# The second norm of two feed-forward blocks, rearranged to one tile per unit of the output projection

## The chip, the cores and the metric

The kernel runs on one core of a Trainium2 chip. The metric is the device time of one execution in microseconds (us), the median of several. A core has five engines with a queue each, worked off in order: TensorE (PE, matrix products; its weight loads are shown apart as PEld), VectorE (DVE), ScalarE (ACT), GpSimd (POOL) and SyncE (SP, which here issues most of the DMA transfers). Engines wait for each other through semaphores. Matrix products are written to PSUM, in eight banks of 128 x 512 fp32 values; all other operands lie in SBUF.

## The reference, cut to what matters

One decoder layer over 2048 prompt positions and 32 sample positions (8 sequences of 4), model width 1024. What concerns the change is the end of the layer:

```python
x = x + jnp.concatenate([att, u * gate], axis=-1) @ w_out          # output projection, residual
h = x * rsqrt(mean(x * x, -1) + EPS) * norm2_g                     # second norm
x = x + (silu(h @ w_gate) * (h @ w_up)) @ w_down                   # feed-forward, width 2816
y = rmsnorm(x, final_g)
```

All of it is fp32. The kernel keeps fp32 accuracy with products of a reduced type: each operand is split into a high half (a rounded copy) and a low half (the operand less its high half), and each product is made of three matmuls, high by high, high by low and low by high.

## The kernel before

The first part (projections, attention, gating) isn't touched. After it the 16 prompt tiles of 128 positions go through in three blocks: tiles 0 to 5, 6 to 11, and 12 to 15 with the sample rows as a fifth, small tile. `next_block` (L1856) runs blocks two and three. Within it a block goes through these steps on TensorE:

1. the last down products of the block before (`downs`);
2. `open_unit` (L1789) for each tile: the first 512 columns of the output projection, 8 steps of 3 matmuls, into one bank per tile (`B.banks`);
3. `second_unit` (L1794) for each tile: the other 512 columns, 24 matmuls (16 for the sample tile) into two alternating banks (`ps_o`);
4. the transposes of the second norm, woven between the units of step 3;
5. the feed-forward over 22 chunks of 128 hidden columns. Its products come as seven products a chunk (`product`, L1564) of sums of quarters of the tiles (a scheme of Strassen's kind: quarters b11, b12, b21, b22 and the sums t1 to t4), so the transposed and scaled tile isn't enough: the norm must also make the four sums and split all seven terms into halves. Block two does its first chunk in two parts, tiles 0 to 3 and tiles 4 and 5.

Every engine works in the order in which the program issues to it. The order around step 3 comes from a small planner: `tick()` (L1267) advances a counter, and `later(n, fn, ...)` (L1263) puts a function off by n ticks. A unit has two ticks, one ahead of each half. At the ticks of step 3 the splits of the first chunk's weights also fall due (`prepare`, L1538: high half on ScalarE at L1513, low half at L1517 on VectorE or GpSimd), and, in block two's second unit and ahead of it, the ends of the last open units (`first_end`, L1851).

The second norm of one tile, as it stands, is four functions:

- `norm2_a` (L1401), issued right after the unit's residual add (`out_end`, L1375): the square of the second half of the row with its sum, on ScalarE (L1405). The first half's sum was made at `first_end`. The scratch output of the square goes where the tile's projection input lay.
- `rms_b` (L1385), one tick later: two small VectorE instructions and the root (Sqrt) on ScalarE (L1389).
- `norm2_b` (L1416), two ticks later: the reciprocal and its refinement on VectorE (`newton`, L142 to L146), then the scaled tile on ScalarE (L1420), into `pair`, which has two buffers.
- `norm2_c` (L1425), `put_off` ticks after that (2, or 1 for a block's last three tiles): eight transposes on TensorE into the two banks of `ps_t` (L1434), three copies out of PSUM on ScalarE (L1449, L1450, L1452), low halves and four sums on VectorE (L1451, L1442 to L1445, L1454), and the high halves of the sums on ScalarE with their low halves on GpSimd (`split_sb`, L135 and L138). The sums lie in `zn` buffers, of which there are three; a tile takes two.

The tick puts `norm2_c` of a tile into the queues two units behind its own, ahead of the root or the scaling of later tiles. In block three the sample tile is the first in the order, but its `norm2_c` stands behind all units (L1896), for its operands take columns 64 to 67 of every quarter of every tile, and the projection inputs of tiles that have not been multiplied lie across these columns (`place_of`, L1323).

Of the kernel before, what the change touches and what calls it, by code (L numbers as in the profile page):

```python
# [64 lines left out]
def hymba_step(ctx: ExitStack, tc: tile.TileContext, A: dict, O: dict):  # L65
# [100 lines left out]
    def zn_tile():  # L166
        return rp.tile([P, 512], F32, name="zn", tag="zn", bufs=3)
# [1105 lines left out]
    class Block:  # L1273
# [6 lines left out]
            self.acc, self.wo, self.cat, self.late, self.h, self.open, self.s1 = {}, {}, {}, {}, {}, {}, {}  # L1280

        def place(self):
            self.X = []
            for nm in ("xh2", "xl2"):
                t_ = fc.tile([P, 6 * 28 * 64], F32R, name=nm, tag=nm)
                self.X.append(t_[:, 0:self.nt * 28 * self.w].rearrange("p (i n) -> p i n", i=self.nt))
            self.ops = [x.rearrange("p i (j k w) -> p i j k w", j=7, k=4) for x in self.X]

    def acc_tile(B, i):
# [32 lines left out]

    def place_of(B, i):  # L1323

        return tuple(x[:, i, 0:KD * P].rearrange("p (s t) -> p s t", t=P) for x in B.X)


# [94 lines left out]

            later(put_off, norm2_c, B, i, xn)

    def norm2_c(B, i, xn):  # L1425

        n = B.rows[i]
        hi, lo_ = B.ops
        pts = []
        for kk in range(2):  # L1430
            pt = ps_t()
            for k in range(4):
                c0 = (kk * 4 + k) * P
                pe.transpose(pt[:, k * P:k * P + n], xn[:n, c0:c0 + P], ident[:n, :n])  # L1434
            pts.append(pt.rearrange("p (k t) -> p k t", k=4)[:, :, 0:n].rearrange("p k (z t) -> p z k t", z=2))
        (b11, b12), (b21, b22) = ((p_[:, 0], p_[:, 1]) for p_ in pts)
        sums = [zn_tile()[:, 0:2 * 4 * (n // 2)].rearrange("p (j k t) -> p j k t", j=2, k=4) for _ in range(2)]
        (t1, t2), (t3, t4) = ((s_[:, 0], s_[:, 1]) for s_ in sums)

        def sums_of():  # L1440

            dve.tensor_sub(t1, t4, b11)  # L1442
            dve.tensor_sub(t3, b22, t4)
            dve.tensor_sub(t2, b22, t1)
            dve.tensor_sub(t4, b21, t2)  # L1445

        if n == P:
            at_ = lambda x, j0, j1: x[:, i, j0:j1, :, 0:64]
            act.activation(at_(hi, 0, 1)[:, 0], b11, AF.Copy)  # L1449
            act.activation(t4, b12, AF.Copy)  # L1450
            dve.tensor_sub(at_(lo_, 0, 1)[:, 0], b11, at_(hi, 0, 1)[:, 0].bitcast(F32))  # L1451
            act.activation(at_(hi, 1, 3), pts[1], AF.Copy)  # L1452
            sums_of()
            dve.tensor_sub(at_(lo_, 1, 3), pts[1], at_(hi, 1, 3).bitcast(F32))  # L1454
            for s_, j in zip(sums, (3, 5)):
                split_sb(at_(hi, j, j + 2), at_(lo_, j, j + 2), s_)
        else:
            act.activation(t4, b12, AF.Copy)
            sums_of()
            for j, x in enumerate((b11, b21, b22, t1, t2, t3, t4)):  # L1460
                at_ = lambda y: y[:, :, j, :, 64:].rearrange("p i k c -> p k i c")
                x = x.rearrange("p k (i c) -> p k i c", i=B.nt)
                split_sb(at_(hi), at_(lo_), x, eng_lo=dve)

# [389 lines left out]
    def next_block(B, downs, finals):  # L1856
# [26 lines left out]
        for i in order:  # L1883
            open_unit(B, i)
        first_operands(B)
        for i in order[:-1] if B.last else order:
            second_end(B, i, second_unit(B, i), 1 if i in tiles[-3:] else 2)
        if B.last:
            i = order[-1]
            out_end(B, i, 1, second_unit(B, i))  # L1890
            s1 = B.s1.pop(i)
            act.activation(B.X[0][:, i, 512:1024], B.acc[i][:, 512:1024], AF.Square, accum_out=s1[:, 3:4])
            rms_b(s1, P, s1[:, 3:4])
            norm2_b(B, i, s1, 2)
            tick()
            norm2_c(B, n - 1, B.xns)  # L1896
            tick()

    for bi, B in enumerate(blocks):
        if bi == 0:  # L1900
# [180 lines left out]
```

## Time and profile before

| what | value |
|---|---|
| median of 3 runs | 2550.32 us (2549.67 to 2557.51) |
| profiled execution, its own time | 2553.33 us |
| span of its profile, first to last instruction | 2551.4 us |
| TensorE busy | 2447.2 us, 96% of the span |
| VectorE, ScalarE, GpSimd busy | 1275.1, 1129.6, 1292.2 us |
| mean granted clock of TensorE | 0.984 |
| block two, first second unit to the first chunk's second part | 1533.0 to 1589.7 us |
| block three, first second unit to the end of the first chunk's second product | 2113.3 to 2161.2 us |

In the profile a row of a timeline has the start in us from the span's start, the duration in us, the engine, the line, the operation, the output and inputs by name, the shapes, a count of merged instructions, and in brackets the idle time ahead of it with the instruction that ended it. A row of a table of stretches has the stretch and its length, then busy time and number of instructions of PE, PEld, DVE, ACT and POOL, the granted clock of TensorE, the share of the DMA engines that was busy and the GB/s that they moved. Matmuls are pipelined, so the duration of one is longer than the distance between two.

### The profile page before, as it was taken

The page shows a single profiled execution, that of the slowest core. Times are in us where ns is not written, and L with a number is a line of the kernel's source. Part 1 is how long each engine was busy: PE and PEld are TensorE (multiplying, and loading weights), DVE is VectorE, ACT ScalarE, POOL GpSimd, SP SyncE. Part 2 cuts the span into 40 slices and gives each one's busy share as a digit, 9 for nine tenths or more (in the row PEclk, how much of TensorE's full clock was granted, in tenths as well). Part 3 has the DMA queues.
Part 4 walks back from the last instruction along what each step waited for, and adds up shares of the span by engine and source line. Part 5 has one row for each costly group of instructions (what it writes and reads, how often), then busy time and mean ns, then how long its engine had stood idle before and what let it go on. Part 6 is the DMA issues. An engine that isn't in the chain of part 4 may idle for free.

```text
span 2551.4 us, 39141 instructions
## 1 busy us (share of the span) xinstructions
PE 2447.2 (96%) x14022; PEld 2120.1 (83%) x14022; DVE 1275.1 (50%) x2598; ACT 1129.6 (44%) x2438; POOL 1292.2 (51%) x1012
## 2 busy tenths in 40 slices
PE   8999999999999898999999999999999998999997
PEld 6777786667888678899899988999999986999996
DVE  4448674216777644443444465444444465444445
ACT  6414333226666556545445355332323345444432
POOL 2116442004777636667677543553645534666662
PEclk9999999999999899999999999999999998999998
DMA  8964735675554463536546471563544543665552
GB/s 260 281 220 150 255 115 164 200 252 197 174 178 151 116 205 112 182 128 198 169 143 201 139 220 62 203 214 128 204 163 160 203 152 122 224 206 192 197 193 106
DMA packets 292149, 455.37 MB, mean 178 GB/s; under 512 B 28695, under 2 KB 160968, under 8 KB 286836
## 3 DMA queue, kind: packets, MB, share of 16 engines
q1 hardware_dynamic: 285108, 440.82, 52.7%
q10 hardware_dynamic: 6848, 12.06, 1.6%
q8 instruction: 111, 1.82, 0.3%
q14 instruction: 82, 0.67, 0.1%
HBM read 365.07 MB, written 157.84 MB: 205 GB/s over the span
## 4 chain that ended last, share of the span: by engine, by line
PE 55%; POOL 9%; issue 7%; ACT 4%; DVE 4%; DMA 2%; SPq 0%; POOLq 0%; ACTq 0%; DVEq 0%
PE ps_o L1647 13%; PE ps_m L1576 8%; PE ps_m L1575 8%; PE ps_m L1574 8%; POOL op L1517 3%; PE ps_s L853 2%; PE ps_o L908 2%; DMA ab_d<-pair 2%; ACT fr L1485 1%; PE ps_t L880 1%; PE ps_s L932 1%; POOL pair L1497 1%; POOL pair L1506 1%; POOL fr L1500 1%; POOL dw L138 1%
## 5 line engine op out<-in xcount | busy, mean ns | idle before, releaser
L1517 POOL TENSOR_TENSOR op<-fr,op 128x512 fp32r<-128x512 f32 x385 | 488.3, 1297 | 313.2 <-ACT op L1513 291.6
L1574 PE MATMUL ps_m<-xh,op 128*128 128x384 f32 (+3 forms) x1904 | 605.2, 318 | 0.0
L1575 PE MATMUL ps_m<-xl,op 128*128 128x384 f32 (+3 forms) x1904 | 604.2, 317 | 0.9 <-POOL xl L138 0.9
L1576 PE MATMUL ps_m<-xh,op 128*128 128x384 f32 (+3 forms) x1904 | 604.6, 318 | 0.0
L1647 PE MATMUL ps_o<-dw,hw 128*128 128x512 f32 x2040 | 484.0, 392 | 15.7 <-DVE acc L1649 14.4
L1647 PEld LDWEIGHTS ps_o<-dw,hw 128*128 128x128 f32 x2040 | 379.5, 188 | 98.6 <-DVE acc L1649 20.7
L1575 PEld LDWEIGHTS ps_m<-xl,op 128*128 128x128 f32 x1904 | 360.3, 189 | 4.8 <-POOL xl L138 1.1
L1574 PEld LDWEIGHTS ps_m<-xh,op 128*128 128x128 f32 x1904 | 360.7, 189 | 4.0
L1576 PEld LDWEIGHTS ps_m<-xh,op 128*128 128x128 f32 x1904 | 360.1, 189 | 0.1
L1649 DVE TENSOR_TENSOR acc<-acc,ps_o 128x512 f32<-128x512 f32 (+1 forms) x362 | 247.1, 686 | 214.8 <-PE ps_o L1647 214.8
L1614 ACT ACTIVATE ps_t<-zn 128x384 f32<-128x384 f32 (+1 forms) x126 | 58.3, 463 | 462.1 <-DVE zn L1597 361.9
L1513 ACT ACTIVATE op<-fr 128x512 fp32r<-128x512 f32 x396 | 235.7, 623 | 24.4 <-DMA fr<-ab_d 19.7
L138 POOL TENSOR_TENSOR dw<-fd,dw 128x1024 fp32r<-128x1024 f32 x66 | 158.5, 2402 | 121.7 <-ACT dw L135 121.7
L318 PE MATMUL ps_s<-wh,xh 128*128 128x512 f32 x480 | 199.7, 416 | 10.6 <-ACT xh L135 6.0
L319 PE MATMUL ps_s<-wl,xh 128*128 128x512 f32 x480 | 191.7, 399 | 1.8 <-DVE wl L226 1.8
L320 PE MATMUL ps_s<-wh,xl 128*128 128x512 f32 x480 | 191.3, 399 | 0.0
L1517 POOL TENSOR_TENSOR op<-pair,op 128x512 fp32r<-128x512 f32 x63 | 81.4, 1301 | 116.4 <-ACT op L1513 116.4
L318 PEld LDWEIGHTS ps_s<-wh,xh 128*128 128x128 f32 x480 | 92.5, 193 | 54.2 <-issue 23.7
L536 POOL TENSOR_TENSOR pr<-kv,qb 96x512 f32<-96x512 f32 x32 | 47.2, 1479 | 178.1 <-DMA qb<-zs_d 61.6
L1624 ACT ACTIVATE hw<-ps_t 128x384 fp32r<-128x384 f32 (+1 forms) x126 | 56.1, 453 | 175.1 <-DVE ps_t L1620 174.1
L924 POOL CAST sq<-k 128x512 fp32r<-128x512 f32 x32 | 34.0, 1062 | 164.3 <-PE ps_s L319 164.3
L320 PEld LDWEIGHTS ps_s<-wh,xl 128*128 128x128 f32 x480 | 92.3, 192 | 20.6 <-DVE xl L138 0.3
(456 smaller groups left out, 4296.6 us busy)
## 6 DMA issues: line engine op xcount, KB each, us to landing
fr<-ab_d SPq DMA_DIRECT2D x308, 256.0 KB
fd<-in_w_down_dram SPq DMA_DIRECT2D x66, 512.0 KB
out_ks_dram<-in_cache_k_dram SPq DMA_DIRECT2D x56, 512.0 KB
out_vs_dram<-in_cache_v_dram SPq DMA_DIRECT2D x56, 512.0 KB
ab_d<-fr SPq DMA_DIRECT2D x88, 256.0 KB
raw<-in_w_in_dram SPq DMA_DIRECT2D x72, 256.0 KB
qk_d<-pair SPq DMA_DIRECT2D x64, 256.0 KB
ab_d<-pair SPq DMA_DIRECT2D x63, 256.0 KB
```

The lines of the kernel that those rows point to most:

```text
L138: (eng_lo or pool).tensor_sub(lo, src, hi.bitcast(F32))
L318: pe.matmul(o[j], xh[:, k, :], wh, start=(k == 0), stop=False)
L319: pe.matmul(o[j], xh[:, k, :], wl, start=False, stop=False)
L320: pe.matmul(o[j], xl[:, k, :], wh, start=False, stop=(k == KD - 1))
L1513: act.activation(ops[f, j][0], ab[f][j], AF.Copy)
L1517: (pool if f or j in POOL_LOW else dve).tensor_sub(lo_, ab[f][j], hi.bitcast(F32))
L1574: pe.matmul(out, wh[:, ks], xh[:, :, k], start=(k == 0), stop=False)
L1575: pe.matmul(out, wh[:, ks], xl[:, :, k], start=False, stop=False)
L1576: pe.matmul(out, wl[:, ks], xh[:, :, k], start=False, stop=(k == 3))
L1614: act.activation(g, c, AF.Silu)
L1647: pe.matmul(ps[0:nr], l_, r_[:, cs], start=(z == 0 and y == 0), stop=(z == FC - 1 and y == len(pairs) - 1))
L1649: dve.tensor_add(B.acc[i][0:nr, cs], B.acc[i][0:nr, cs], ps[0:nr])
```

## The change

`norm2_c` is cut into three parts: `norm2_t`, the transposes, which can now be given their banks; `norm2_v`, the copies out of PSUM; and `norm2_s`, the low halves, sums and splits. A new function `chain` issues, for tile i whose unit has just been issued: the residual add, the square, `rms_b`, the copies of the tile in front, the refinement of the root, the scaling of tile i, and then the sums and splits of the tile in front. Nothing of that is put off by ticks.

In `next_block` the loop over the units issues a unit, then the transposes of the tile in front, then `chain`. Every other tile's transposes go into the banks `ps_m` 0 and 1, which the open units have left, and the rest into `ps_t` as before. The last tile of block two is finished four ticks later, behind three products of the first chunk, with the banks of `ps_o`; the last tile of block three at once, with its low halves on VectorE and not on GpSimd, and the ring of product banks is set so that the first product takes `ps_m` 2. In block three the sample tile's `second_end` comes first, as before, but its `norm2_c` stands behind the first prompt tile's unit and chain. So that it can, the projection inputs of block three's tiles 1 to 3 move to the end of the operand buffers, which that block leaves free (`B.rest`).

```diff
         def place(self):
-            self.X = []
+            self.X, self.rest = [], []
             for nm in ("xh2", "xl2"):
                 t_ = fc.tile([P, 6 * 28 * 64], F32R, name=nm, tag=nm)
                 self.X.append(t_[:, 0:self.nt * 28 * self.w].rearrange("p (i n) -> p i n", i=self.nt))
+                self.rest.append(t_[:, self.nt * 28 * self.w:])
...
     def place_of(B, i):
 
+        if B.last and i:
+            return tuple(x[:, (i - 1) * D:i * D].rearrange("p (s t) -> p s t", t=P) for x in B.rest)
         return tuple(x[:, i, 0:KD * P].rearrange("p (s t) -> p s t", t=P) for x in B.X)
...
-    def norm2_c(B, i, xn):
+    def norm2_t(B, i, xn, banks=None):
 
         n = B.rows[i]
-        hi, lo_ = B.ops
         pts = []
         for kk in range(2):
-            pt = ps_t()
+            pt = banks[kk]() if banks else ps_t()
...
+        return pts
+
+    def norm2_v(B, i, pts):
+
+        n = B.rows[i]
+        (b11, b12), _ = ((p_[:, 0], p_[:, 1]) for p_ in pts)
+        sums = [zn_tile()[:, 0:2 * 4 * (n // 2)].rearrange("p (j k t) -> p j k t", j=2, k=4) for _ in range(2)]
+        if n == P:
+            hi = B.ops[0][:, i, :, :, 0:64]
+            act.activation(hi[:, 0], b11, AF.Copy)
+        act.activation(sums[1][:, 1], b12, AF.Copy)
+        if n == P:
+            act.activation(hi[:, 1:3], pts[1], AF.Copy)
+        return sums
+
+    def norm2_s(B, i, pts, sums, eng_lo=None):
+
         (b11, b12), (b21, b22) = ((p_[:, 0], p_[:, 1]) for p_ in pts)
...
+        if B.rows[i] == P:
+            hi, lo_ = (x[:, i, :, :, 0:64] for x in B.ops)
+            dve.tensor_sub(lo_[:, 0], b11, hi[:, 0].bitcast(F32))
+        dve.tensor_sub(t1, t4, b11)
+        dve.tensor_sub(t3, b22, t4)
+        dve.tensor_sub(t2, b22, t1)
+        dve.tensor_sub(t4, b21, t2)
+        if B.rows[i] == P:
+            dve.tensor_sub(lo_[:, 1:3], pts[1], hi[:, 1:3].bitcast(F32))
             for s_, j in zip(sums, (3, 5)):
-                split_sb(at_(hi, j, j + 2), at_(lo_, j, j + 2), s_)
...
+                split_sb(hi[:, j:j + 2], lo_[:, j:j + 2], s_, eng_lo=eng_lo)
+            return
...
+    def norm2_c(B, i, xn, banks=None, eng_lo=None):
+        pts = norm2_t(B, i, xn, banks)
+        norm2_s(B, i, pts, norm2_v(B, i, pts), eng_lo)
+
+    def chain(B, i, ps, ahead):
+
+        out_end(B, i, 1, ps)
+        s1 = B.s1.pop(i)
+        act.activation(place_of(B, i)[0][:, 4:8], B.acc[i][:, 512:1024].rearrange("p (s t) -> p s t", t=P), AF.Square,
+                       accum_out=s1[:, 3:4])
+        rms_b(s1, P, s1[:, 3:4])
+        if ahead:
+            sums = norm2_v(B, *ahead)
+        r = rms_c(s1, P)
+        xn = square_tile()
+        act.activation(xn, B.acc[i], AF.Copy, scale=r)
+        if ahead:
+            norm2_s(B, *ahead, sums)
+        return xn
...
         first_operands(B)
-        for i in order[:-1] if B.last else order:
-            second_end(B, i, second_unit(B, i), 1 if i in tiles[-3:] else 2)
         if B.last:
-            i = order[-1]
-            out_end(B, i, 1, second_unit(B, i))
...
-            norm2_c(B, n - 1, B.xns)
-            tick()
+            second_end(B, n - 1, second_unit(B, n - 1))
+        two = lambda fn, *a: [lambda: fn(*a[0:1]), lambda: fn(*a[1:2])]
+        front = None
+        for i in tiles:
+            ps = second_unit(B, i)
+            ahead = None
+            if front:
+                ahead = (front[0], norm2_t(B, *front, two(ps_m, 0, 1) if (front[0] + B.last) % 2 else None))
+            front = i, chain(B, i, ps, ahead)
+            if B.last and i == tiles[0]:
+                norm2_c(B, n - 1, B.xns)
+        if B.last:
+            norm2_c(B, *front, eng_lo=dve)
+            turn[3] = 1
+        else:
+            later(4, norm2_c, B, *front, two(ps_o))
```

30 lines of the change are left out of this document (4 added, 26 removed).

## The prediction

> **What bounds the kernel now.** I read the page first, then a table of stretches around the two stages that the change touches, then TensorE's timeline in them, then the rows of the engines that TensorE waits for.
>
> ```profile
> PE 2447.2 (96%) x14022; PEld 2120.1 (83%) x14022; DVE 1275.1 (50%) x2598; ACT 1129.6 (44%) x2438; POOL 1292.2 (51%) x1012
> ```
>
> TensorE is the bound over the span. The stretches, by TensorE busy time, the other engines, granted clock and DMA share:
>
> ```profile
> 1572.00:1589.70 17.70, 14.48 (x100) 14.28 (x101) 9.30 (x26) 9.05 (x18) 5.02 (x4) 0.81 0.00 1
> 2113.30:2145.50 32.20, 30.11 (x137) 23.72 (x135) 15.47 (x45) 16.73 (x34) 9.30 (x8) 0.95 0.38 132
> 2145.50:2161.20 15.70, 7.60 (x42) 6.37 (x40) 8.10 (x30) 10.12 (x26) 5.14 (x5) 0.67 0.00 1
> ```
> ```profile
> 1590.00:1650.00 60.00, 60.00 (x354) 57.07 (x354) 26.36 (x50) 22.53 (x44) 31.75 (x23) 1.00 0.54 184
> 2161.20:2220.00 58.80, 58.80 (x422) 56.07 (x421) 27.95 (x65) 28.54 (x64) 43.70 (x32) 1.00 0.63 215
> ```
>
> Right behind each stage TensorE is full at clock 1.00. In the second norms it is not, and the clock falls to 0.81 and 0.67. So time won there should reach the end. TensorE in block two (a unit is the 24 matmuls of one tile's second half of the output projection; T(i) the eight transposes of tile i; q0 to q6 the seven products of the first feed-forward chunk):
>
> ```profile
> 1532.99 0.39 PE L1367 MATMUL ps_o<-woh,xh 128*128 128x512 f32 x1
> ...
> 1546.59 1.03 PE L1434 MATMUL ps_t<-ident,pair 128*128 128x128 f32 x8
> ...
> 1565.26 1.09 PE L1434 MATMUL ps_t<-ident,pair 128*128 128x128 f32 x8 [2.23 <-ACT pair L1420]
> ...
> 1571.91 1.09 PE L1434 MATMUL ps_t<-ident,pair 128*128 128x128 f32 x8
> 1572.76 0.36 PE L1574 MATMUL ps_m<-xh,op 128*128 128x256 f32 x1
> ...
> 1579.09 1.97 PE L1434 MATMUL ps_t<-ident,pair 128*128 128x128 f32 x8 [3.22 <-ACT pair L1420]
> 1580.71 0.56 PE L1574 MATMUL ps_m<-xh,op 128*128 128x256 f32 x1
> ...
> 1589.81 0.28 PE L1575 MATMUL ps_m<-xl,op 128*128 128x128 f32 x1
> ```
>
> T(3) waits 2.23 us and T(5) 3.22 us for the scaled tile (pair); after the second wait everything runs at about half speed. Prices: two and a half units from 1532.99 to 1546.59, so 5.44 us a unit; T 0.85 us (1571.91 to 1572.76), or 1.62 us at the low clock (1579.09 to 1580.71); q0 and q1 end at 1579.09 - 3.22 = 1575.87 with 0.16 us of drain, so 1.45 us a product. The same in block three, where tile 4 is the sample tile S:
>
> ```profile
> 2113.32 0.39 PE L1372 MATMUL ps_o<-woh,cats 128*64 128x512 f32 x1
> ...
> 2116.95 0.39 PE L1367 MATMUL ps_o<-woh,xh 128*128 128x512 f32 x1
> ...
> 2136.61 1.09 PE L1434 MATMUL ps_t<-ident,pair 128*128 128x128 f32 x8 [2.08 <-ACT pair L1420]
> ...
> 2144.69 1.03 PE L1434 MATMUL ps_t<-ident,pair 128*128 128x128 f32 x8
> ...
> 2150.67 0.60 PE L1434 MATMUL ps_t<-ident,xns 32*128 32x32 f32 x4 [4.94 <-DVE zn L1442]
> 2154.16 2.16 PE L1434 MATMUL ps_t<-ident,pair 128*128 128x128 f32 x8 [1.16 <-DVE xl L138]
> 2155.96 0.57 PE L1574 MATMUL ps_m<-xh,op 128*128 128x272 f32 x1
> ...
> 2159.88 0.39 PE L1575 MATMUL ps_m<-xl,op 128*128 128x272 f32 x1 [0.88 <-POOL xl L138]
> ```
>
> T(1) waits for its tile; T(S) and then T(3) wait for readers of the two transpose banks; q1 waits for GpSimd's low halves.
>
> **Why the scaled tile is late.** VectorE in block two, around tile 3, and ScalarE's scaling of it:
>
> ```profile
> 1557.60 0.68 DVE L1378 TENSOR_TENSOR acc<-acc,ps_o 128x512 f32<-128x512 f32 x1
> ...
> 1563.12 0.15 DVE L142 RECIPROCAL s<-s 128x1 f32<-128x1 f32 x1
> ```
> ```profile
> 1564.06 1.15 ACT L1420 ACTIVATE pair<-acc,s 128x1024 f32<-128x1024 f32 x1 [0.72 <-DVE s L146]
> ```
>
> From the residual add to the scaled tile it takes 1565.21 - 1557.60 = 7.6 us, because the root's four small instructions stand behind the sums of an earlier tile. Block three's last tile has that chain free of sums:
>
> ```profile
> 2144.89 0.69 DVE L1378 TENSOR_TENSOR acc<-acc,ps_o 128x512 f32<-128x512 f32 x1 [2.87 <-PE ps_o L1369]
> ...
> 2147.04 0.16 DVE L142 RECIPROCAL s<-s 128x1 f32<-128x1 f32 x1 [0.27 <-ACT s L1389]
> ...
> 2147.74 0.21 DVE L146 TENSOR_SCALAR s<-s 128x1 f32<-128x1 f32 x1
> ```
> ```profile
> 2146.80 0.20 ACT L1389 ACTIVATE s<-s 128x1 f32<-128x1 f32 x1 [0.47 <-DVE s L1388]
> 2148.05 1.15 ACT L1420 ACTIVATE pair<-acc,s 128x1024 f32<-128x1024 f32 x1 [1.04 <-DVE s L146]
> ```
>
> Counted from the transposes that follow the unit (2144.69), the add starts at 0.2, the root (Sqrt) ends at 2.3, its refinement at 3.3, the scaling at 4.5 us.
>
> **The change, part by part.** (1) Order within a unit. Each unit's chain now comes whole, with T of the tile in front ahead of it on TensorE. Put into the chain are that tile's three copies out of PSUM (after the root, before the scaling); its sums follow on VectorE. Their cost, from tile 3 before:
>
> ```profile
> 1566.01 0.38 ACT L1449 ACTIVATE xh<-ps_t 128x256 fp32r<-128x256 f32 x1 [0.19 <-PE ps_t L1434]
> ...
> 1566.56 0.61 ACT L1452 ACTIVATE xh<-ps_t 128x512 fp32r<-128x512 f32 x1
> 1568.16 1.15 ACT L135 ACTIVATE xh<-zn 128x512 fp32r<-128x512 f32 x2 [0.99 <-DVE zn L1444]
> ```
> ```profile
> 1566.70 0.42 DVE L1451 TENSOR_TENSOR xl<-ps_t,xh 128x256 fp32r<-128x256 f32 x1 [2.09 <-ACT zn L1450]
> ...
> 1568.50 0.68 DVE L1454 TENSOR_TENSOR xl<-ps_t,xh 128x512 fp32r<-128x512 f32 x1
> ```
> ```profile
> 1568.87 2.54 POOL L138 TENSOR_TENSOR xl<-zn,xh 128x512 fp32r<-128x512 f32 x2 [3.48 <-ACT xh L135]
> ```
>
> Copies 1.16 us, sums 2.48 us, two high halves 1.15 us starting 1.46 us after the sums, two low halves on GpSimd 0.7 us later, 2.54 us. In the new order the copies run from 2.3 to 3.5, the scaling to 4.65; TensorE asks for that tile after T and the next unit, at 0.85 + 5.44 = 6.3. Slack 1.6 us, so no wait. VectorE starts the sums at 3.3 and ends at 5.8; one weight low half of 128x512, priced like L1454 at 0.68, makes it 6.5, when the next add is due (6.3 + 0.2). ScalarE: high halves to about 5.9, two weight high halves, priced like the pair of L135 at 1.15, to 7.1, next square at 7.2. Both engines just fit; a few tenths over eat slack and are not seen by TensorE. No instruction is added, no DMA is moved.
>
> (2) Block two ends with T(4), q0, q1, q2, then T(5): TensorE asks for T(5) at 0.85 + 4.35 = 5.2 against 4.65. No wait. VectorE then works off tile 5's sums behind q1 and q2, and q4's second add, which frees q3's bank, comes about 12 us after T(4) began, when TensorE wants that bank: 0.3 us. New time of the first 128-wide product: 1532.99 + 6 x 5.44 + 6 x 0.85 + 7 x 1.45 + 0.3 = 1581.2, against 1589.7 before. **Gain 8.5 us.**
>
> (3) Block three, sample tile moved ahead of unit 1. TensorE wants T(S) at 2116.95 + 5.44 = 2122.4, but
>
> ```profile
> 2122.45 1.14 ACT L1420 ACTIVATE xns<-acc,s 32x1024 f32<-32x1024 f32 x1
> ```
>
> ends at 2123.6, and nothing ahead of it moves: a new wait of 1.2 us. T(S) costs at most the 0.85 us of a whole tile. Its small splits, 2.4 us alternating between ScalarE and VectorE at the end of the stage before, now lie under unit 1. For this the layout puts the projection inputs of tiles 1 to 3 elsewhere; same transfers, other addresses, no cost. Unit 3 then ends at 2123.65 + 0.85 + 3 x 5.44 + 2 x 0.85 = 2142.5.
>
> (4) Block three's tail. Nothing is left to put ahead of T(3). From T(2) at 0: T(3) at 4.7 (an idle of 3.7 us, longer than block two's 3.22, so I take the low clock), ending at 6.3. Tile 2's first low half on GpSimd ends at 6.7, and tile 3's second copy needs that zn buffer (three buffers, two a tile), so its first low product operand is there at 7.5; q0, at the low clock before (from 2155.96 to 2159.88 - 0.88 less the drain, 2.8 us), ends at 10.3; tile 3's low halves are on VectorE now, the one that q1 wants at 10.2; q1 (1.45 x 272/256 = 1.54 us) ends at 11.9, at 2154.4. Before, it ended at 2159.88 + 11/12 x 1.54 = 2161.3. **Gain 6.9 us.**
>
> (5) Other banks. In block two TensorE's waits name only the scaled tile: worth nothing there. In block three the banks and the move of S remove the waits of 4.94 and 1.16 us, counted in (4). The product banks 0 and 1 that T(1) and T(3), or T(0) and T(2), use are read out 0.7 us or more before q0 writes, and after T(2) the ring is set so that q0 takes banks 2 and 3 first: no wait.
>
> Sum 15.4 us. The profiled execution took 2553.33 us around its span of 2551.4, 3.0 us over the median; the median 2550.3 less 15.4 is **2534.9 us**.
>
> **The clock.** Two stretches of 3.41 us ahead of the first drops, and one where there was none:
>
> ```profile
> 1574.48:1577.89 3.41, 1.39 (x12) 1.18 (x10) 2.97 (x12) 1.63 (x5) 1.84 (x2) 1.00 0.00 0
> ```
> ```profile
> 2134.26:2137.67 3.41, 1.32 (x11) 1.06 (x10) 1.60 (x6) 2.50 (x6) 2.49 (x2) 1.00 0.00 0
> ```
> ```profile
> 1560.82:1564.23 3.41, 2.21 (x10) 1.50 (x8) 3.27 (x11) 1.69 (x4) 1.33 (x2) 1.00 0.00 0
> ```
>
> TensorE busy 1.3 to 1.4 us of such a stretch brought the low clock, 2.2 us did not; a gap of 1.2 us (part 3) should not. The Trainium skill, "TensorE: Matmul & The Clock Gate" ("Part 1: The HAM clock gate"), has the clock halve after an idle window of 3.4 us; by it the gap of 2.08 us would have been free, which this trace denies. The Trainium skill, same page ("Part 4: PE-mode transpose"), also says that transposes do not count as busy for the gate, which no stretch here separates; by that sentence the low clock of the tail would last into q1 and q2, and the time would be some 2 us later, an estimate from that page, at 2537, inside the forecast's own range.
>
> **Rivals.** *ScalarE or VectorE paces the units* (0.2). For: part 1 leaves them tenths. Against: 1.6 us of slack per unit. If hops and the weight halves stretch a unit by 2.5 us, four units of block two and two of block three lose 0.9 us each, 5.4 us: 2540. *The gain doesn't reach the end* (0.1, half of it for block three alone). If GpSimd, 43.70 of 58.80 us busy behind block three, sets the next chunks, block three's 6.9 us are given back: 2541.8; were both stages, no change. Against: TensorE is full in both stretches after. *The order on the engines stays as crowded as it is* (0.05): the change then doesn't do what it says, and T(3) and T(5) go on waiting as the 7.6 us chain has them wait, 2550. Against: the emission order is written out, and the root stands ahead of the sums in it. *Slower* (0.04): the chain stays at tile 3's 7.6 us or longer behind copies that wait for a zn buffer, and each wait over 2 us brings the low clock. Block three's wait of 2.08 us cost 1.6 us more at the low clock (0.05 of 32.20 us), 3.7 a unit; eight units lose 30 us against 15 won: 2565. It decides once a chain ends 8.3 us after T instead of 4.65. Against: only tile 3's second copy meets a buffer still in use by the working of part 4.
>
> **How the numbers follow.** As worked out 0.61, within 2531 to 2538.5: a gain up to 4 us larger if the tail keeps its clock (1.5 us) and GpSimd's buffer and the S wait cost nothing (2 us), up to 3.6 us smaller if half clock lasts to q2 and T(5) waits 1 us. With the first two rivals the range is **2531 to 2543**. What a measurement can tell from no change is 0.3%, 7.7 us: faster 0.61 + 0.2 + 0.05 = 0.86, same 0.05 + 0.05 = 0.1, slower 0.04.
>
> **What would show it.** Between the units of block two no idle of TensorE and clock 1.00 up to the 128-wide products; the root's RECIPROCAL ahead of the sums on VectorE in each unit; T(S) behind unit 0 with a wait of about 1.2 us; one idle of 3 to 4 us ahead of T(3) and one low-clock stretch. Wrong would be a wait for pair ahead of T(0) to T(2), a low clock in block two, or TensorE under 97% busy in the 60 us behind a stage.

## The result, and the profile after

The changed kernel takes 2536.91 us (median of 4 executions, 2534.39 to 2537.98) where the kernel before took 2549.99 (4 executions beside it): a ratio of 0.9943, 95% interval 0.9924 to 0.9961 (the comparison's own estimate; the quotient of the two medians is 0.9949). Two more comparisons of the same kernel, with more executions, gave 0.9938 (0.9921 to 0.9956) and 0.9946 (0.9924 to 0.9967). The forecast was 2534.9 us in a range of 2531 to 2543. One execution of a later experiment ran at a mean granted clock of 0.61 and is left out of its comparison.

By stages the profiled execution (2534.39 us, span 2532.2) says more than the total. A stage starts at its first matmul of a second unit; block two's ends at the first 128-wide product, block three's at VectorE's add behind q1. The kernel before ended them here:

```profile
1589.75 0.22 PE L1574 MATMUL ps_m<-xh,op 128*128 128x128 f32 x1
```
```profile
2161.63 0.44 DVE L1586 TENSOR_TENSOR raw<-raw,ps_m 128x272 f32<-128x272 f32 x1 [2.77 <-PE ps_m L1576]
```

The same marks in the timelines of TensorE and VectorE after, with the transposes T(1), T(4) and T(5) of block two, and T(S), T(2) and T(3) of block three:

```profile
1530.17 0.39 PE L1370 MATMUL ps_o<-woh,xh 128*128 128x512 f32 x1
...
1547.39 1.03 PE L1436 MATMUL ps_m<-ident,pair 128*128 128x128 f32 x8
...
1566.39 1.03 PE L1436 MATMUL ps_t<-ident,pair 128*128 128x128 f32 x8
...
1571.58 1.03 PE L1436 MATMUL ps_o<-ident,pair 128*128 128x128 f32 x8
...
1578.74 0.30 PE L1603 MATMUL ps_m<-xh,op 128*128 128x128 f32 x1 [0.38 <-DVE zn L1624]
...
2102.00 0.39 PE L1375 MATMUL ps_o<-woh,cats 128*64 128x512 f32 x1
...
2112.30 0.68 PE L1436 MATMUL ps_t<-ident,xns 32*128 32x32 f32 x8 [1.07 <-ACT xns L1423]
...
2131.15 1.03 PE L1436 MATMUL ps_m<-ident,pair 128*128 128x128 f32 x8
2135.64 1.09 PE L1436 MATMUL ps_t<-ident,pair 128*128 128x128 f32 x8 [3.46 <-ACT pair L1489]
```
```profile
2142.54 0.44 DVE L1615 TENSOR_TENSOR raw<-raw,ps_m 128x272 f32<-128x272 f32 x1 [1.38 <-PE ps_m L1605]
```

| | before | after | won |
|---|---|---|---|
| block two's second norm | 1532.99 to 1589.75, 56.8 us | 1530.17 to 1578.74, 48.6 us | 8.2 |
| from there to block three's second norm | 523.6 us | 523.3 us | 0.3 |
| block three's second norm | 2113.32 to 2161.63, 48.3 us | 2102.00 to 2142.54, 40.5 us | 7.8 |
| from there to the end of the span | 389.7 us | 389.7 us | 0.0 |

Together 16.3 us. The two spans differ by 19.1; the other 2.8 us lie ahead of 1530 us, where both kernels do the same. That front part varies: over the thirteen profiles compared below, block two's stage started anywhere from 1527.3 to 1538.3 us, while its length, wherever its code was the changed kernel's, repeated within 0.05 us. So the stages, and not the spans, are compared below.

The table of stretches after: block two's stage, block three's up to T(2) and from there on, then the same lengths behind each stage as the prediction showed of before. The columns are busy time of PE, PEld, DVE, ACT and POOL, clock, DMA share and GB/s.

```profile
1530.17:1578.74 48.57, 48.20 (x277) 42.08 (x276) 30.81 (x88) 30.52 (x64) 19.25 (x15) 1.00 0.22 72
2102.00:2131.15 29.15, 28.08 (x137) 22.31 (x136) 16.74 (x55) 17.88 (x42) 7.91 (x7) 1.00 0.45 152
2131.15:2142.54 11.39, 7.10 (x44) 6.40 (x43) 7.92 (x22) 8.23 (x19) 5.39 (x5) 0.85 0.00 0
1579.00:1639.00 60.00, 60.00 (x354) 57.07 (x354) 26.89 (x51) 22.93 (x45) 32.09 (x24) 1.00 0.53 184
2142.50:2201.30 58.80, 58.80 (x420) 56.02 (x419) 28.10 (x65) 29.37 (x64) 43.72 (x32) 1.00 0.65 220
```

Block two's stage is full but for 0.37 us, at clock 1.00. Behind both stages TensorE is as full as before, so nothing was given back. What is left to win in these two stages lies mostly in the 11.4 us of block three's tail. The table of waits from 2095 to 2150 us names it (us in total, times, longest):

```profile
PE ps_t L1436 <- ACT pair L1489: 3.5, 1, 3.5
PE ps_t L1436 <- ACT xns L1423: 1.1, 1, 1.1
PE ps_m L1603 <- ACT xh L1447: 0.5, 1, 0.5
PE ps_m L1604 <- DVE xl L1459: 0.3, 1, 0.3
```

The waits for readers of the transpose banks (4.94 and 1.16 us before) and for GpSimd's low halves (0.88) are gone. This is how a unit's chain now looks on VectorE and on ScalarE, for the unit that ended with T(1) at 1547.39:

```profile
1548.16 0.68 DVE L1381 TENSOR_TENSOR acc<-acc,ps_o 128x512 f32<-128x512 f32 x1
...
1550.30 0.17 DVE L142 RECIPROCAL s<-s 128x1 f32<-128x1 f32 x1 [0.27 <-ACT s L1392]
...
1551.13 0.41 DVE L1459 TENSOR_TENSOR xl<-ps_m,xh 128x256 fp32r<-128x256 f32 x1
```
```profile
1550.17 0.37 ACT L1447 ACTIVATE xh<-ps_m 128x256 fp32r<-128x256 f32 x1
...
1551.25 1.16 ACT L1489 ACTIVATE pair<-acc,s 128x1024 f32<-128x1024 f32 x1
```

From the add to the scaled tile it takes 1552.41 - 1548.16 = 4.25 us instead of 7.6. The sums of the tile in front come behind the refinement of the root, and the scaling runs beside them.

### The profile page after: what moved, and what is told of

It reads as the page before. It is cut to its first block, busy times and chain, and to the rows that moved or that the text cites. A ratio compares the mean times of both kernels' runs of the same rounds, so it can differ in the third digit from the quotient of the medians.

```text
span 2532.2 us, 39133 instructions
## 1 busy us (share of the span) xinstructions
PE 2434.5 (96%) x14022; PEld 2109.2 (83%) x14022; DVE 1277.6 (50%) x2600; ACT 1130.3 (45%) x2438; POOL 1291.5 (51%) x1010
## 4 chain that ended last, share of the span: by engine, by line
PE 56%; POOL 8%; issue 7%; DMA 3%; DVE 3%; ACT 3%; SPq 0%; POOLq 0%; ACTq 0%; DVEq 0%
PE ps_o L1676 13%; PE ps_m L1603 8%; PE ps_m L1604 8%; PE ps_m L1605 8%; POOL op L1546 3%; PE ps_s L853 2%; PE ps_o L908 2%; DMA ab_d<-pair 2%; ACT fr L1514 1%; PE ps_t L880 1%; PE ps_s L932 1%; POOL pair L1526 1%; POOL fr L1529 1%; PE ps_s L318 1%; POOL dw L138 1%
```

## The experiments

The theory: what wins is the order inside the chain (refinement and scaling ahead of the sums of the tile in front), on both stages. The rivals: that it is the chain's not being put off by ticks, whatever its inner order; that the other banks carry it; that the sample tile's new place carries block three; that the low clock in the tail, and not the chain, is what is left. Four kernels, each with one profiled execution, take the change apart. The rest ask whether the same order also pays in block one.

| kernel | block two's stage | block three's stage | low clock in the latter |
|---|---|---|---|
| before | 56.8 | 48.3 | 13.6 |
| changed (three profiles) | 48.6, 48.6, 48.6 | 40.5, 40.7, 40.9 | 3.4, 6.8, 6.8 |
| sums first | 56.9 | 46.7 | 10.2 |
| same banks | 48.8 | 40.6 | 3.4 |
| sample late | 48.6 | 41.9 | 6.8 |
| filled hole | 48.6 | 40.4 | none |

### Sums of the tile in front first

```diff
-            sums = norm2_v(B, *ahead)
+            norm2_s(B, *ahead, norm2_v(B, *ahead))
         r = rms_c(s1, P)
         ...
-        if ahead:
-            norm2_s(B, *ahead, sums)
```

> The units, their transposes and the banks stay as in the changed kernel; within a unit the sums of the tile in front go ahead of the refinement of the root and of the scaling on VectorE and ScalarE. Stage two is read from the first matmul of its second units to the first 128-wide product (48.6 us in the changed kernel), stage three from its first second unit to VectorE's add behind the second product (40.5 us). Theory (the gain is that the root and the scaling stand ahead of the sums): the scaled tile is ready 7.9 us after the transposes began in place of 4.65, and TensorE asks at 6.3, so a wait of about 1.6 us at the first tile that has one in front, tenths at the next ones, about 1.2 us ahead of the last transposes: stage two 51.7 us; in stage three 1.6 us at one unit and some 2 to 3 us at the end: 44 us. Rival (the gain is that the chain follows its unit at once and is no longer put off by ticks; the order within it doesn't matter): both stages within 0.5 us of the changed kernel.

Block two's stage takes 56.88 us, block three's 46.70. The waits of TensorE in both, and the place in block two where the order shows (VectorE's last sum, then the root of the next tile, then ScalarE's scaling):

```profile
PE ps_m L1436 <- ACT pair L1489: 3.4, 2, 2.5
PE ps_o L1436 <- ACT pair L1489: 2.1, 1, 2.1
PE ps_t L1436 <- ACT pair L1489: 0.8, 1, 0.8
```
```profile
PE ps_t L1436 <- ACT pair L1489: 6.4, 2, 5.3
PE ps_m L1436 <- ACT pair L1489: 2.5, 1, 2.5
```
```profile
1547.60 0.68 DVE L1465 TENSOR_TENSOR xl<-ps_t,xh 128x512 fp32r<-128x512 f32 x1
1548.20 0.15 DVE L142 RECIPROCAL s<-s 128x1 f32<-128x1 f32 x1
```
```profile
1549.14 1.15 ACT L1489 ACTIVATE pair<-acc,s 128x1024 f32<-128x1024 f32 x1 [0.72 <-DVE s L146]
```

The theory's direction holds and its size was too small: the whole 8.2 us of block two is lost, and 6.2 of block three's 7.8, though the banks, the one-tile distance and the absence of ticks are all still there. That rules out the rival: issuing the chain at once wins nothing in block two without the order inside it. (Whether the order would win as much if the chain were still put off by ticks was not run.) The loss grows beyond the forecast because a late scaling holds up what stands behind it on ScalarE, the weights' high half, and with it VectorE's low half and then the next tile's residual add, which starts 1.9 us after T(2), where the forecast of the chain has 0.2:

```profile
1558.22 1.45 DVE L1544 TENSOR_TENSOR op<-fr,op 128x512 fp32r<-128x512 f32 x1 [1.74 <-ACT op L1540]
```

The wait of 2.5 us that follows brings the low clock besides. In block three this kernel still wins 1.6 us on the kernel before: that is what all the rest of the change (banks, the sample tile's place, no ticks, the last low halves on VectorE) is worth together when the sums come first.

### The banks, the sample tile's place, the idle in the tail

```diff
-ahead = (front[0], norm2_t(B, *front, two(ps_m, 0, 1) if (front[0] + B.last) % 2 else None))
+ahead = (front[0], norm2_t(B, *front))
 ...
-            later(4, norm2_c, B, *front, two(ps_o))
+            later(4, norm2_c, B, *front)
```

> As the changed kernel, but every tile's transposes go into the two banks of ps_t. Theory (the order carries the gain, the banks little of it): stage two 49 to 49.6 us in place of 48.6, from waits of about 0.4 us ahead of T(3) and 0.5 us ahead of T(5) for the reads of the tile in front; stage three 41.7 us in place of 40.5, since the last transposes wait 1.2 us for the sums of tile 2. Rival (the other banks are what took away the waits of 4.94 and 1.16 us that stood in block three): stage three 44 us or more.

48.76 and 40.62 us. The one new wait is in the tail, where T(3)'s second bank is still being read:

```profile
PE ps_t L1436 <- DVE xl L1465: 0.6, 1, 0.6
```

The banks are worth 0.2 us in block two and 0.1 in block three, less than either side expected. In this order two banks are enough.

```diff
-            if B.last and i == tiles[0]:
-                norm2_c(B, n - 1, B.xns)
         if B.last:
+            norm2_c(B, n - 1, B.xns)
             norm2_c(B, *front, eng_lo=dve)
```

> As the changed kernel, but the sample tile's transposes and splits go back behind all units, ahead of the last tile's transposes. Theory (the move is worth little beside the new order): the wait of 1.1 us and the transposes' 0.6 us leave the front of stage three, and the last transposes wait for the sample tile's alternating splits, which end about 2.9 us after the changed kernel's last transposes began: stage three 1.2 us longer, 41.7 us in place of 40.5. Rival (the move is what took away the old wait of 4.94 us): stage three longer by 5 us or more, 45.5 us. Stage two the same, 48.6 us, by both.

Block three's stage takes 41.93 us, 1.4 more than in the changed kernel's first profile. T(3) waits longer, for the sample tile's splits, and the low clock lasts 6.8 us:

```profile
PE ps_t L1436 <- DVE xl L138: 5.9, 1, 5.9
```

Against the five profiles of the changed kernel's block three in which the low clock also lasted 6.8 us (40.7 to 41.8), the move is worth 0.2 to 1.2 us. The rival of 5 us is out.

```diff
         if B.last:
+            fill = ps_m(3)
+            for _ in range(14):
+                pe.matmul(fill, B.cat[front[0], 0][0], B.wo[1, 0][0], start=True, stop=True)
             norm2_c(B, *front, eng_lo=dve)
```

> As the changed kernel, but 14 matmuls of 128x512 into a product bank that nobody reads stand between the last unit's transposes of tile 2 and those of tile 3 in block three: 3.2 us of work that is not needed, in the idle of 3.46 us. Theory (the end of stage three is bound by the last tile's chain on ScalarE and VectorE, and the low clock behind the idle costs little): the last transposes begin at the same time, the first product runs at the full clock and the second then waits for VectorE's low half; stage three 40.0 us in place of 40.5. Rival (the low clock of 3.41 us is what is paid there): stage three 1.7 us shorter, 38.8 us.

The 14 matmuls' product is not used. They stand in the idle ahead of T(3), which now waits only 0.3 us; the clock is 1.00 through the stage; and the stage takes 40.44 us, 0.1 less than in the changed kernel:

```profile
PE ps_m L1604 <- DVE xl L138: 0.7, 1, 0.7
...
PE ps_t L1436 <- ACT pair L1489: 0.3, 1, 0.3
```

With the full clock, q1 waits 0.7 us for the low halves of tile 3, which VectorE makes: the tail is bound by the chain of the last tile, and the low clock of 3.4 us hides behind it. Seven profiles below and above have the changed kernel's code in block three: two with 3.4 us of low clock took 40.5 and 40.6 us, five with 6.8 us 40.7 to 41.8. Against the 40.44 us at full clock that is 0.1 to 1.3 us, according to where the low clock falls.

### The same order in block one

In the changed kernel block one keeps the old order. "Stage one" is from the first of block one's last six second units to its first 128-wide product, "behind" from there to block two's stage. TensorE's waits for scaled tiles in it, after:

```profile
PE ps_t L1436 <- ACT pair L1423: 6.7, 3, 4.7
```

Beside five ways to give block one the order, the changed kernel ran twice more. The four kernels of the experiments above have its code in block one too, and with them the sum runs from 609.5 to 612.1 us:

| kernel | stage one | behind | sum | ratio to before |
|---|---|---|---|---|
| changed, three profiles | 64.4, 62.7, 62.8 | 547.0, 547.0, 546.8 | 611.4, 609.8, 609.6 | 0.9943, 0.9938, 0.9946 |
| tiles 1, 3, 4, 5 | 63.7 | 551.9 | 615.5 | 0.9956 (0.9938 to 0.9973) |
| tiles 3, 4, 5 | 60.3 | 550.6 | 610.9 | 0.9929 (0.9912 to 0.9947) |
| the same, last low halves on VectorE | 62.4 | 553.3 | 615.8 | 0.9949 (0.9933 to 0.9965) |
| all six tiles | 62.6 | 549.7 | 612.3 | 0.9945 (0.9930 to 0.9961) |
| all six, two adds moved | 59.7 | 551.9 | 611.6 | 0.9938 (0.9925 to 0.9951), 0.9932 (0.9912 to 0.9951) |

The changed kernel, no edit:

> The changed kernel again, unaltered, timed in more rounds beside the kernel before. Theory (15 to 16 us are won in the two stages and nothing is given back): ratio 0.994, some 2535 against 2550 us; stages 48.6 and 40.5 us. Rival (part is given back behind the stages): the stages the same, but the stretch between them longer than the 523.6 us of the kernel before, and the ratio nearer to 1.

> The changed kernel as it is, beside the run before on the same chip, to settle whether block one's order is worth anything. By stages: one and the stretch behind it together 609 to 612 us, second norms of blocks two and three 48.6 and 40.5 to 40.7 us, ratio to the kernel before 0.9925 to 0.9955; rival, that the two earlier ratios owed something to their chips: outside of that.

2536.01 and 2536.64 us, and every stage within 0.3 us of what was expected (block three's took 40.7 and 40.9 us, and 523.3 us lay between the two stages both times); the rival that one chip made the ratio is out.

**Tiles 1, 3, 4 and 5**, and block three's sample transposes in the middle of unit 1:

```diff
-        second_end(B, 1, p1)
-        p3 = second_unit(B, 3)
-        open_end(B, 3)
-        second_end(B, 3, p3)
 ...
+        norm2_half(B, 1)
+        front = 1, chain(B, 1, p1, None)
+        for i in (3, 4, 5):
+            ps = second_unit(B, i)
 ...
+            ahead = front[0], norm2_t(B, *front, [lambda: ps_m(0), lambda: ps_m(1)] if i == 4 else None)
+            front = i, chain(B, i, ps, ahead)
```

> The changed kernel with the same order in block one for its tiles 1, 3, 4 and 5 (chain and transposes one unit apart, other banks for tile 3, the last tile four ticks later), and with the sample tile's transposes in the middle of the unit behind the one they follow now. Stage one is read from the first second-half unit of block one to the first 128-wide product (64.4 us in the changed kernel); it has TensorE waits of 1.5, 4.7 and 0.5 us for scaled tiles and 6.8 us of low clock. Theory (the same cause works there): stage one 56 to 57 us, stage three 39.5 us (its wait of 1.07 us gone), the whole about 9 us under the changed kernel, ratio to the kernel before 0.9905. Rival (in block one ScalarE also multiplies the weights by the gain, eight instructions of 0.3 us at a tick, and becomes the pace): stage one 61 us or more, ratio 0.992 to 0.994.

2540.51 us. The waits for scaled tiles are gone from the stage, but the transposes of tiles 0, 2 and 1 now met and waited 6.4 us in all for readers of their banks (the 9.0 us in the expectation after this one counts 2.6 us too many), and the stretch behind grew by 4.9 us. Block three's stage took 40.3 us and not 39.5: without the wait of 1.07 us the tail's idle was longer, 4.25 us.

**Tiles 3, 4 and 5 alone**: as above, with `second_end(B, 1, p1)` kept and the chain from tile 3 on.

> Block one's tiles 3, 4 and 5 alone in the order root, scaling, sums of the tile in front (tile 1 as in the changed kernel, sample transposes behind the first prompt unit again). In the run with all blocks the transposes of three tiles met ahead of tile 3's unit and waited 9.0 us for readers of their banks; tile 1 is now back where it was. Theory: that meeting is gone, the waits of 6.7 us for scaled tiles go, and the first norm stage, 64.4 us in the changed kernel (62.7 in its second profile), takes 56 to 58 us; but GpSimd ends the last tile's low halves as late as in the run with all blocks (there it took up the next chunk's weight sums 0.6 us after the stage's end, where the changed kernel took them up 2.0 us before), so the stretch from the end of stage one to the start of stage two grows again from 547.0 to 550 to 552 us. Net gain over the changed kernel 2 to 5 us, ratio to the kernel before 0.992 to 0.993. Rival, that VectorE and ScalarE are full in that stage whatever the order: stage one stays at 61 or more, ratio 0.994 to 0.996.

2535.77 us. Stage one came between theory and rival, the stretch behind as the theory had it. T(2) ended at 949, but its copies queued on ScalarE behind tile 3's scaling and the half squares of tiles 4 and 5, so that T(1) waited 5.3 us:

```profile
955.58 0.36 ACT L1447 ACTIVATE xh<-ps_t 128x256 fp32r<-128x256 f32 x1
```
```profile
957.14 0.45 PE L1436 MATMUL ps_t<-ident,pair 128*128 128x128 f32 x1 [5.34 <-DVE zn L1460]
```

And behind the stage GpSimd is late. It takes up the weights' sums at 984.00 us instead of 981.16, for stages that end at 983.4 and 983.2; in the first chunk it has only pauses of 1.8, 0.9 and 0.5 us, so that it is still 2.8 us late at 1006.7, and a product waits for it. This wait is 2.2 of the 3.6 us by which the stretch behind grew:

```profile
1008.01 0.45 PE L1605 MATMUL ps_m<-xh,op 128*128 128x384 f32 x1 [2.15 <-POOL op L1546]
```

**The last tile's low halves on VectorE**, to spare GpSimd:

```diff
-        later(4, norm2_c, B, *front, [ps_o, ps_o])
+        later(4, norm2_c, B, *front, [ps_o, ps_o], dve)
```

> As the run before, with the low halves of block one's last tile on VectorE instead of GpSimd. Theory: GpSimd takes up the next chunk's weight sums 2.5 us earlier, the stretch from stage one to stage two is back at 547 to 548.5 us, stage one grows by at most 1.3 us against the run before (VectorE's two low halves of 0.64 us stand ahead of its adds of the first products); ratio 0.990 to 0.992. Rival, that the stretch behind grows for another reason than GpSimd's late start (the low clock alone, or the weights' high halves on ScalarE): it stays at 550 to 552 us, ratio as in the run before.

2541.35 us. The wait for GpSimd is gone, as the theory had it, and the stretch behind is longer still: VectorE's adds of the first products came late, TensorE waited 3.2 us ahead of the 128-wide products and then ran at half clock for 20.5 us. Theory and rival both missed that.

**All six tiles**, every one with its chain behind its unit:

```diff
-        second_end(B, 0, second_unit(B, 0))
+        x0 = chain(B, 0, second_unit(B, 0), None)
         open_end(B, 2)
-        second_end(B, 2, p2, 3)
+        x2 = chain(B, 2, p2, None)
 ...
+        front = 1, chain(B, 1, p1, (0, norm2_t(B, 0, x0)))
 ...
         open_end(B, 3)
 ...
+        for i in (3, 4, 5):
+            ps = second_unit(B, i, (lambda: norm2_c(B, 2, x2, second(1))) if i == 3 else None)
```

> All six tiles of block one in the order root, scaling, sums of the tile in front, with tile 2's transposes in the middle of unit 3 and with every second tile's transposes in product banks that the open units have left; nothing of the norm is put off by ticks, and no copies of a tile queue behind another tile's half squares (in the run with tiles 3 to 5 alone the copies of tile 2 came 7.5 us after its transposes and held TensorE for 5.3 us). Theory, that the waits moved forward because tiles 0 to 2 kept the old order: no wait of TensorE for bank readers over 1 us, no low clock in the stage, stage one 51 to 54 us against 62.7 to 64.4 in the changed kernel and 60.3 with tiles 3 to 5 alone; the stretch behind it grows from 547.0 to 550.5 to 552 us, as it did there. Ratio to the kernel before 0.988 to 0.991. Rival, that VectorE and ScalarE have too much to do in that stage (weights' high halves and sums besides): stage one stays at 58 or more, ratio 0.992 to 0.994.

2538.78 us. The theory failed by my own edit: the residual add that frees unit 1's bank stood behind the other tile's root, the mistake that this change mends elsewhere.

```profile
934.71 0.68 DVE L1381 TENSOR_TENSOR acc<-acc,ps_o 128x512 f32<-128x512 f32 x1
```
```profile
935.44 0.79 PE L1370 MATMUL ps_o<-woh,accm 128*128 128x512 f32 x1 [5.61 <-DVE acc L1381]
```

**The two adds moved** (against the kernel with all six tiles; `chain` leaves out the add when it gets no bank):

```diff
-        x0 = chain(B, 0, second_unit(B, 0), None)
+        p0 = second_unit(B, 0)
+        out_end(B, 2, 1, p2)
+        out_end(B, 0, 1, p0)
         open_end(B, 2)
-        x2 = chain(B, 2, p2, None)
+        x0 = chain(B, 0, None, None)
+        x2 = chain(B, 2, None, None)
+        open_end(B, 3)
 ...
-        open_end(B, 3)
```

> As the run before with two adds moved: the residual add of tile 2, which frees the bank that unit 1 wants, ahead of tile 0's chain and not behind its root, and the add of tile 3's first half ahead of unit 1's chain. In the run before TensorE waited 5.6 us and 2.3 us for these two adds. Theory, that those waits are all that held stage one up: they fall to 2 us and to nothing, the low clock of 10.2 us in the stage with them, stage one takes 51 to 54 us against 62.6; the stretch behind it is 547 to 550 us where the clock holds, and 555 to 556 where the idle of 1.0 us ahead of the 128-wide products brings the low clock, which in the run before lasted 17.1 us, until the 384-wide products came. Ratio to the kernel before 0.988 to 0.991. Rival, that ScalarE's extra weight work of this block (two groups of 2.4 us) sets the pace: stage one stays at 57 or more, ratio 0.992 to 0.994.

> The kernel of the run before once more, since its profiled execution ran at a clock of 0.61 throughout and its stages can't be read: as expected there, stage one 51 to 54 us and the stretch behind it 547 to 550 us where the clock holds, 555 to 556 where it falls ahead of the 128-wide products. By the six undisturbed executions of the run before (2530.9 to 2537.9 us) the total gains at most 2 us on the changed kernel, so I now lean to the clock falling: stage one and the stretch behind it together 606 to 610 us, against 609.8 and 611.4 in the changed kernel's two profiles.

2535.84 us, then 2533.70. The wait of 5.6 us is gone, and stage one takes 59.7 us: the rival was right. In block one ScalarE also multiplies the next weights by the norm's gain, eight instructions in a row ahead of a tile's square, and the scaled tiles are late again (from the table of waits in the stage, then ScalarE's rows):

```profile
PE ps_o L1436 <- ACT pair L1495: 1.9, 1, 1.9
```
```profile
965.98 2.44 ACT L1520 ACTIVATE fr<-fr,g2c 128x128 f32<-128x128 f32 x8
968.33 1.04 ACT L1489 ACTIVATE xh<-acc 128x1024 fp32r<-128x1024 f32 x1
```

The 3 us won in the stage are lost behind it (5 us, with a wait of 2.2 us for GpSimd again and 10.2 us at half clock), and the sum of 611.6 us misses the 606 to 610 expected of the second run. So none of the five can be told from the changed kernel as faster: the best median is 3 us lower, with intervals that overlap. How much of the growth behind the stage is GpSimd's late start and how much the clock was not separated; they don't simply add, for with all six tiles half clock lasted 17.1 us, no product waited for GpSimd, and the growth, 2.7 us, was the smallest of the five.

## Why the prediction was right, and where it was off

*Part 1, the order within a unit.* Right: no wait between units, clock 1.00, the root's RECIPROCAL ahead of the sums, and the experiment with the sums first gives back all of block two's gain and 6.2 us of block three's. The scaled tile came 5.0 us after T(1) began, where 4.65 was forecast, and TensorE asked for it at 6.34 (6.3). The slack of 1.6 us was 1.3: a weight low half on VectorE took 1.62 us and not 0.68, so the add came at 0.8 instead of 0.2. The rival that VectorE and ScalarE pace the units was this near, and in block one, with 2.4 us more for ScalarE in a unit, it came true.

*Part 2, block two's end.* T(5) was asked for 5.19 us after T(4) (forecast 5.2), the idle ahead of the 128-wide products was 0.38 us (0.3), the stage 48.6 us (48.2), the gain 8.2 (8.5). The 0.4 us are small prices read too low: a unit with its transposes took 6.33 us where the sum has 6.29, and a product 1.47 (three from 1567.18 to 1571.58) where it has 1.45; the prediction's own rows, (1575.87 - 0.16 - 1572.76) / 2, give 1.475.

*Part 3, the sample tile.* The new wait was 1.07 us (1.2), and T(2), which stands behind unit 3, came 29.15 us after the stage's start (29.2).

*Part 4, block three's tail.* The sum was near, 11.4 us from T(2) to the end of q1 where 11.9 was forecast, but two terms in it were wrong. The idle was 3.46 us (3.7) and the low clock did come, but only behind T(3). And tile 3's second copy didn't wait for a `zn` buffer: ScalarE's own queue held it, behind the splits of tile 2, and it ran while GpSimd was still at that tile's first low half. These rows are from ScalarE and GpSimd:

```profile
2135.76 1.15 ACT L135 ACTIVATE xh<-zn 128x512 fp32r<-128x512 f32 x2 [0.17 <-DVE zn L1462]
...
2137.09 0.38 ACT L1448 ACTIVATE zn<-ps_t 128x256 f32<-128x256 f32 x1
```
```profile
2136.47 2.51 POOL L138 TENSOR_TENSOR xl<-zn,xh 128x512 fp32r<-128x512 f32 x2 [3.06 <-ACT xh L135]
```

So q0 started 6.1 us after T(2) and not 7.5. T(3) ran at the full clock, but q0, at the low clock as forecast, took 3.4 us with 0.3 of waiting where 2.8 was forecast. That the sum came within 0.5 us all the same is in part luck. The gain of the stage was 7.8 us in the profile shown and 7.4 to 7.6 in the two others, where 6.9 was forecast.

*Part 5, the banks.* Worth nothing in block two was right (0.2 us). In block three I put the end of the 4.94 and 1.16 us waits down to banks and move. Undone one at a time they cost 0.1 and at most 1.4 us, and with the sums first they win at most 1.6 together with the rest of the change. So the order, which reads the banks sooner, seems to remove most of those waits by itself; that is not shown, for both undone at once was not run.

*The clock.* Windows of 3.41 us with TensorE busy for 1.3 to 1.4 us brought the low clock before, 2.2 us didn't. The tail after fits, in the two windows ahead of the place where the clock falls, 2137.5:

```profile
2130.67:2134.08 3.41, 1.52 (x11) 1.12 (x9) 2.12 (x7) 2.22 (x8) 2.50 (x2) 1.00 0.07 27
2134.08:2137.49 3.41, 1.34 (x9) 1.04 (x9) 2.64 (x8) 3.24 (x7) 1.01 (x1) 1.00 0.00 0
```

1.52 us kept the full clock and 1.34 lost it. No edge between them follows: ahead of these stages a window of 1.67 us was followed by the low clock (before, 885.00 to 888.40), and one of 1.62 was not (after, 949.60 to 953.00), so from 1.5 to 1.7 us the busy time alone does not tell. The price of the low clock, 1.5 us in the forecast's range, was 0.1 in this profile, for it lay beside the chain. That transposes do not count as busy for the gate in the way that other matmuls do (the Trainium skill, "TensorE: Matmul & The Clock Gate", "Part 4: PE-mode transpose") would have kept the low clock into q1 and q2. It ended at 2140.9, where q0 did, and in the other two profiles 3.4 us later, so no run here decides it; those two stages were 0.2 to 0.4 us longer, not 2.

*The end.* TensorE was full behind both stages, so the gains reached the end, and the rival that GpSimd takes them back didn't come in blocks two and three; in block one it did. The slower rival's mechanism is partly real (with the sums first both waits of 2.5 us in the units brought the low clock, one of 2.1 didn't, and the total only came back to where it was), but its place was not reached: the chain ended at 5.0 us, not 8.3. The sum of the two gains was 15.4 us in the forecast and 15.6 to 16.0 in the three profiles; the medians differ by 13.1, 14.4 and 15.4 us.

## What to carry to other kernels

On engines that work in order, put what produces TensorE's next operand ahead of what finishes the tile before, even where that leaves the finishing work late: here 2.5 us of sums moved behind a root were worth 8 us in one stage and 6 in the other. Before the same order is copied to another stage, ask of each engine in turn what else it has to do there, and which add or copy that frees a bank now stands behind the chain: in block one ScalarE and GpSimd had no room, and each repair moved the wait to another engine. And compare stages, whose lengths repeat to tenths, where the front of the program moves the total by several us.

## What the runs showed of the hardware that was not expected

A subtraction of two SBUF operands of 128x512 takes VectorE 0.69 us alone. Begun while GpSimd was subtracting SBUF operands, it took 1.62, and GpSimd's pair 3.01 instead of 2.50 (VectorE's row first, alone in the kernel with the sums first and then beside GpSimd in the changed one; then GpSimd's rows, beside that instruction, and beside VectorE instructions with only one operand in SBUF, from 2130.91):

```profile
1540.65 0.69 DVE L1544 TENSOR_TENSOR op<-fr,op 128x512 fp32r<-128x512 f32 x1
```
```profile
1546.61 1.62 DVE L1546 TENSOR_TENSOR op<-fr,op 128x512 fp32r<-128x512 f32 x1
```
```profile
1546.38 3.01 POOL L138 TENSOR_TENSOR xl<-zn,xh 128x512 fp32r<-128x512 f32 x2 [4.43 <-ACT xh L135]
...
2130.91 2.50 POOL L138 TENSOR_TENSOR xl<-zn,xh 128x512 fp32r<-128x512 f32 x2 [2.63 <-ACT xh L135]
```

Half of GpSimd's undisturbed pair is 1.25 us; started at 1546.38 it ends at 1547.63, and 0.6 us later VectorE is done. The numbers are as if each had waited out an instruction of the other. The Trainium skill, "SBUF — State Buffer" ("Who interferes with whom"), states this: a VectorE instruction with two SBUF inputs and a GpSimd instruction that reads SBUF block one another, and the order of issue decides who waits. The trace agrees; the prediction priced that low half at its time alone.

The half clock did not end after a few us of full work where the products were 128 wide. With all six tiles of block one in the new order, an idle of 1.0 us ahead of those products brought it, TensorE was then busy without a gap, and it lasted 17.1 us, into the 384-wide products (the windows before its start, at its start, and behind its end at 1001.1):

```profile
980.60:984.00 3.40, 2.63 (x24) 2.66 (x24) 2.78 (x6) 0.81 (x2) 3.32 (x4) 1.00 0.02 5
984.00:987.40 3.40, 3.40 (x19) 3.40 (x18) 3.40 (x3) 1.12 (x4) 3.25 (x3) 0.51 0.54 202
...
1001.10:1004.50 3.40, 3.40 (x21) 3.40 (x21) 0.56 (x1) 2.05 (x4) 3.40 (x2) 1.00 0.00 0
```

With the last low halves on VectorE it lasted 20.5 us in the same place. In three other kernels the same idle of 1.0 us there did not bring the low clock at all (with tiles 3 to 5 the window 979.90 to 983.30, busy 2.47 us, kept it, where 2.63 lost it here), and at full clock the same products keep it. Why is not settled: that the gate counts a narrow product for less than its time is only a guess.
